# Attention outputs stored from GpSimd's queue, two outputs kept on chip, earlier loads for the first merges

## The chip, the cores and the metric

The kernel runs on one core of a Trainium2 chip. A core has TensorE (PE; PEld is its weight load), VectorE (DVE), ScalarE (ACT) and GpSimd (POOL), which work side by side and wait for each other through semaphores. SyncE (SP) only issues transfers between the chip's memory (HBM) and the on-chip buffers; GpSimd and ScalarE can issue them too. The metric is the device time of one execution in microseconds, the median of several runs.

## The reference

A hybrid decoder block on one sequence of 1024 tokens, width 1024. Queries, keys and values for 24 heads of 64, the convolution's input and two gates come from one projection. The part that the change touches:

```python
DILATED_GROUPS = ((128, 1), (512, 4), (2048, 16))     # three groups of 8 heads

outs, lses = [], []
for g, (window, dilation) in enumerate(DILATED_GROUPS):
    o_g, lse_g = dilated_group_attention(q[:, :, g], k[:, :, g], v[:, :, g], tab, window, dilation)
    outs.append(o_g)
    lses.append(lse_g)
alpha = jax.nn.softmax(jnp.stack(lses, axis=0), axis=0)
o = jnp.einsum('gbsh,gbshd->bshd', alpha, jnp.stack(outs, axis=0))
return o.reshape(B, S, ATTN_OUT_W) @ w_attn_out

u = layer_norm(u, g_ln, b_ln)          # after the depthwise convolution
return silu(u) @ w_conv_out + b_conv_out

merged = sigmoid(z_ga) * y_attn + sigmoid(z_gc) * y_conv
x = x + rms_norm(merged @ w_mix_out, g_post_mix)
h = rms_norm(x, g_pre_ffn)
x = x + rms_norm((silu(gate) * up) @ w_ffn_out, g_post_ffn)    # gate, up = split(h @ w_ffn_in)
```

Every head of the three groups attends along its own dilation, and the three groups' outputs for the same head slot are added with weights from their softmax denominators.

## The kernel before, in words

All matrix products are float32 work done in parts: an operand is split into a rounded high part (ScalarE, a cast) and the low remainder (VectorE or GpSimd, a subtraction), and three products are added. The helper `both` makes such a split with L195 (high part, ScalarE) and L196 (low part); `unit` (L305, L307, L309) issues the three products, tile by tile, for the projections between 840 and 1000 us.

The stages, by the profile's time: the input projections and the Winograd form of the convolution run to about 590 us; the norm after the convolution lies beside their end. From there the value projections (L948 to L952) run, with the attention interleaved, to about 870 us together with the first units of the convolution's output projection. The other units of that projection run to 941 us; each is evicted by L1576 and stored to an HBM buffer `dgc` by L1578, from which L1559 loads it. The attention's output projection follows (evictions L1603), then the mixing projection (L1638), the FFN's input (L321 to L323), and its output (L1909).

The attention works through 12 units, one for each head pair `hp` (0 to 3) and group `g` (0 to 2), in the order g0 for hp 0 and 1, g1 for hp 0 and 1, g2 for hp 0 and 1, and then the same for hp 2 and 3. A unit has 8 steps, one per 128 tokens. A step issues the scores (`att_s`, L1048, bias and maximum on VectorE in L1051), a step behind it the exponentials (`att_e`, L1061), then the transposes (`att_t`, L1086, with copies by L1093 on ScalarE and L1094 on VectorE) and the products with the values (`att_p`, L1121), copied into an output tile `O` by L1141. The stages of a step lag: products come 5 steps after their scores, so that the last product of a unit lies in the next unit. Within a unit GpSimd does the values' low part (`value_parts`, L918 and L922, at steps 4 and 5) and duplicates the next unit's queries onto the other half of the partitions (`double`, L886 and L887, first half at step 6, second half at step 7; the first half is read from the next unit's step 0, the second from its step 4).

When a unit's `O` is complete, L1145 stores it (512 KB, tensor `datt`, one for each g and hp) 3 ticks later, through SP's queue. The softmax statistics of groups 0 and 1 are stored after the last exponential of a unit by `tokens_out` (L1070: 1024 pieces of 16 bytes; L1072: 256 pieces of 64 bytes; tensor `dst`), also on SP, and read back in another order by L891 for the last group's unit.

With group 2 done, a generator `merge(hp, st)` starts. It makes the three groups' weights, stores them (tensor `dw`, L1184) and, once allowed, loads the three outputs (L1193, 512 KB each, in a `b` buffer) and the weights spread over the partitions (`spread`, L1154, two transfers of 256 KB each). It multiplies each output by its weights (L1204, L1208, L1216), adds (L1212, L1221) and splits the sum with `both` (L195, L196) as the operand of the attention's output projection. Until the change a merge's loads wait for the end of the attention (`self.fine is not None`) and for their turn, and four merges follow each other.

The order of the work is written by generators. TensorE's code calls `tick` after every three matmuls; `tick` runs the steps that `later(n, ...)` put n ticks ahead, and advances each background generator (`bg`), which pauses with `yield n` for n ticks. `beat` advances the attention, 0.42 steps of its generator per matmul (0.8 in the convolution's output units). Each engine, and SP's queue, then works strictly in the order written; an instruction that waits holds everything behind it. There are 42 buffers of 4 KB per partition (`b`) and a ring of 3 (`d`) for the outputs `O` and others; a load waits until the readers of the buffer's earlier content are done.

`conv_norm` subtracts the mean from the 8 channel blocks, sums the squares (L1270), makes the reciprocal deviation (`rstd`) and scales. Its steps pause 3 ticks each; when it ends, `normed` becomes 9 and the attention may begin.

Of the kernel before, what the change touches and what calls it, by code (L numbers as in the profile page):

```python
# [62 lines left out]
class Build:  # L63
# [910 lines left out]
    def attention(self):  # L974

        live, s, total = {}, 0, 96
        order = [(g, 2 * hg + i) for hg in range(2) for g in range(3) for i in range(2)]
        nxt, cur, u, x, V = self.stacks(*order.pop(0)), None, 8, None, None
        for i in range(5):
            self.stack_load(nxt)  # L980
        second = self.stacks(*order.pop(0))

        def there():
            return nxt[1] // 2 * 3 + nxt[0] < self.vn

        while s < total + self.LP:
            if s < total:
                if x is None and nxt and there():
                    x = self.values(*nxt[:2])
                if u == 8:  # L990
                    while self.normed < 9 or x is None:
                        if second and second[5] < min(5, self.normed - 4):
                            self.stack_load(second)
                        if x is None and there():
                            x = self.values(*nxt[:2])
                        yield 0
                    if cur is None:
                        self.double(nxt, 0)
                        self.double(nxt, 1)
                    cur, u, nxt, V = nxt, 0, None, []  # L1000
                live[s] = a = {}
                self.att_s(a, cur, V, u)
                u += 1

                if u in (4, 5):
                    if len(V) < 2:
                        V.append(self.value_parts(x, u - 4))
                    if u == 5:
                        x = None
                if u == 6 and cur[0] == 2:  # L1010
                    self.other_stats(cur)
                if u in (6, 7) and nxt:
                    self.double(nxt, u - 6)
                if u == 8:
                    cur[2] = cur[3] = V = None
                if u == 1:
                    if second:
                        nxt, second = second, None
                    elif order:
                        nxt = self.stacks(*order.pop(0))  # L1020
                if nxt and nxt[5] < 5:
                    self.stack_load(nxt)
            if 0 <= s - 1 < total:
                self.att_e(live[s - 1])
            yield 0
            if 0 <= s - self.LT < total:
                self.att_t(live, s - self.LT)
                yield 0
            if 0 <= s - self.LP < total:
                yield from self.att_p(live, s - self.LP)  # L1030
            s += 1
# [34 lines left out]
    def tokens_out(self, g, dst, src):  # L1066

        if g == 0:
            d = dst.rearrange("(u p) e -> p u e", p=128)
            self.nc.sync.dma_start(d, src)  # L1070
        else:
            self.nc.sync.dma_start(dst.rearrange("(b p c) e -> p b (c e)", b=2, c=4),  # L1072
                                   src.rearrange("p (b c) e -> p b (c e)", b=2))

    def att_t(self, live, k):
# [21 lines left out]
    def att_p(self, live, k):  # L1097


        nc = self.nc  # L1100
        a, b, hh = live[k & ~1], live[k | 1], k & 1
        g, hp, u = a["g"], a["hp"], a["u"]
        if hh == 0:
            a["o"] = self.bank("o")
        ps = a["o"]
        hi, lo = a.pop(("pt", hh))

        if g == 2:
            todo = [(u, 0, 128, 0), (u + 1, 128, 128, 128)]
        else:  # L1110
            n = 256 + 128 * (len(a["blocks"]) > 1)
            todo = [(u, 0, 256, 0)] + [(u - 1, 256, 128, 0)] * (n > 256) + [(u + 1, n, 128, 128)]
        for j, (kb, x, n, q) in enumerate(todo):
            kb = self.place(g, kb)
            v, w = a["V"][kb // 4]
            c = (kb % 4) * 256 + hh * 128
            vh = v[:, c:c + 66]
            vl = v[:, c + 64:c + 130] if c < 896 else w
            o = ps[0:66, hh * 256 + q:hh * 256 + q + n]
            for i, (y, z) in enumerate(((vh, hi), (vl, hi), (vh, lo))):  # L1120
                nc.tensor.matmul(o, y, z[:, x:x + n], start=i == 0 and j == 0, stop=i == 2 and j == len(todo) - 1,  # L1121
                                 skip_group_check=True)
            if j < 2:
                yield 0
        hi = lo = v = w = vh = vl = y = z = None
        if hh == 0:
            return
        if u == 0:
            self.O = self.ring()

        O = self.O
        e = (8, 2, 128)[g]
        if g == 0:
            d = O.rearrange("p (c m) -> p m c", c=8)[:, u * 16:u * 16 + 32]
        elif g == 1:
            d = O.rearrange("p (e c m) -> p c m e", e=2, c=4)[:, u // 2]
        else:
            d = O[:, u * 128:u * 128 + 256].rearrange("p (c m) -> p c m", c=2)
        for h in range(2):
            x = ps[0:64, h * 256:(h + 1) * 256]  # L1140
            nc.vector.tensor_copy(d[h * 64:(h + 1) * 64], x.rearrange("p (a e) -> p a e", e=e))  # L1141
        a["o"] = ps = d = x = O = None
        del live[k - 1], live[k]
        if u == 6:
            self.later(3, lambda x=self.O: nc.sync.dma_start(self.d_att[g, hp], x))  # L1145
            if g == 2:
                self.merges.append(self.bg(self.merge(hp, a["p"][4])))
            self.O = None

    def spread(self, hp, g):  # L1150
# [4 lines left out]
                tensor=d.tensor, offset=d.offset + (2 * g + e) * T, ap=[[0, 64], [1, T]]))  # L1155
        return x

    def merge(self, hp, st):

        nc = self.nc  # L1160
        yield 2
# [2 lines left out]
        w = t[:, 32:80].rearrange("p (g u e) -> p g u e", g=3, u=8)  # L1164
# [20 lines left out]
        t = None  # L1185
        yield 4

        while self.fine is not None or hp > self.turn:
            yield 0

        def load(g):
            y = self.slot()
            nc.sync.dma_start(y, self.d_att[g, hp])  # L1193
            return y
# [6 lines left out]
        yield 1  # L1201
        w = self.spread(hp, 1)
        yield 7
        nc.vector.tensor_tensor(y, y, x, op=OP.mult)  # L1204
        x = None
        x = self.spread(hp, 2)
        yield 1
        nc.vector.tensor_tensor(z, z, w, op=OP.mult)  # L1208
        w = None
        w = load(2)  # L1210
        yield 1
        nc.vector.tensor_tensor(y, y, z, op=OP.add)  # L1212
        z = None
        self.turn += 1
        yield 9
        nc.vector.tensor_tensor(w, w, x, op=OP.mult)  # L1216
        x = None
        yield 2
# [5 lines left out]
        yield 2  # L1224
        self.OT[hp] = self.both(z)

    turn = weighed = 0

    def split(self, src, n):
        nc = self.nc  # L1230
# [9 lines left out]
    def conv_norm(self):  # L1240
        nc = self.nc
        mean = self.slot()
        A = []

        def load():
            A.append(self.slot())
            nc.sync.dma_start(A[-1], self.d_conv[len(A) - 1])

        for _ in range(4):
            load()  # L1250
        yield 3
        for hf in range(2):
            s = slice(hf * H, (hf + 1) * H)
            ps = self.bank("s")
            nc.tensor.matmul(ps, self.mean_col.to_broadcast([128, 128]), self.csum[:, s], start=True, stop=True)
            nc.scalar.copy(mean[:, s], ps)
        self.csum = None
        yield 1
        q = []
        for b in range(10):  # L1260
            if b < 4:
                load()
            if b < 8:
                nc.vector.tensor_tensor(A[b], A[b], mean, op=OP.subtract)
            if 0 < b < 9:
                q.append(self.slot())
                nc.scalar.activation(q[-1], A[b - 1], AF.Square)
            if b > 2:
                p = q.pop(0)
                nc.vector.tensor_tensor(q[0], q[0], p, op=OP.add)  # L1270
            p = None
            yield 3
        mean = None
        yield 3
        pb = yield from self.rstd(q[0], T, self.eps_ln, 6)
        rs = self.slot()
        for hf in range(2):
            nc.scalar.copy(rs[:, hf * H:(hf + 1) * H], pb[hf])
        q = None
        for b in range(9):  # L1280
            if b < 8:
                nc.vector.tensor_tensor(A[b], A[b], rs, op=OP.mult)
            if b:
                a, A[b - 1] = A[b - 1], None
                nc.scalar.activation(a, a, AF.Silu, bias=self.col(C_BLN + b - 1), scale=self.col(C_GLN + b - 1))
                self.later(3, lambda b=b, a=a: nc.sync.dma_start(self.d_act[b - 1], a))
                a = None
                self.normed = b
            yield 1
        yield 9  # L1290
        self.normed = 9

    room = False
# [731 lines left out]
```

## Time and profile before

| | us |
|---|---|
| median of 3 runs | 1733.52 (1730.94 to 1735.8) |
| the profiled execution | 1729.18 |
| its span, first to last instruction | 1727.4 |
| TensorE busy | 1699.1 (98%) |
| VectorE, ScalarE, GpSimd busy | 1252.3, 790.1, 462.2 |
| mean granted clock of TensorE | 0.994 |

The rows of a profile name the engine, the line of the kernel, the operation and what it writes and reads (`b<-datt`: from the tensor `datt` into a `b` buffer). A count stands behind an x. In the rows on waits, "A <- B" says that A was idle until B was done. The waits are inferred: where an instruction waits for several things, the one that came last by the profile is named. A row of a window has, for each engine, the busy time and the count of instructions, then the granted clock, the mean busy share of the 16 DMA engines and what they moved.

### The profile page before, as it was taken

How to read it: one execution, taken by the hardware profiler on the slowest of the kernel's cores; microseconds unless marked ns; L12 is line 12 of the kernel's file. 1: busy time of each engine (PE TensorE's matmuls, PEld its weight loads, DVE VectorE, ACT ScalarE, POOL GpSimd, SP SyncE). 2: the span in 40 equal slices, each digit the busy share in tenths (PEclk: the TensorE clock that was granted, in tenths of full speed). 3: DMA queues.
4: the chain of work that ended last, by engine and by line, in shares of the span. 5: the costliest groups of instructions: out<-in, count | busy, mean ns of one | idle time of the engine just before them, and what ended most of it. 6: DMA issues, size and time to landing. Idle time of an engine off the chain costs nothing.

```text
span 1727.4 us, 24529 instructions
## 1 busy us (share of the span) xinstructions
PE 1699.1 (98%) x8758; PEld 1442.1 (83%) x8758; DVE 1252.3 (72%) x2214; ACT 790.1 (46%) x1550; POOL 462.2 (27%) x365
## 2 busy tenths in 40 slices
PE   8999999999999999999998999999999999999998
PEld 7788888888888999999786888888888888888886
DVE  6789978889997657677766755676556555677586
ACT  6344343344444566667622346643333333454463
POOL 0017778887885123434200120000000000000000
PEclk9999999999999999999999999999999999999999
DMA  4352434545578797888789732223322332395244
GB/s 164 111 174 88 156 116 140 160 169 183 169 188 214 223 250 207 234 219 227 224 242 321 272 125 92 90 73 110 129 92 92 110 109 92 135 362 161 92 141 153
DMA packets 167991, 285.52 MB, mean 165 GB/s; under 512 B 52434, under 2 KB 83853, under 8 KB 167869
## 3 DMA queue, kind: packets, MB, share of 16 engines
q1 hardware_dynamic: 167468, 283.46, 52.1%
q8 instruction: 69, 1.13, 0.3%
q14 instruction: 54, 0.43, 0.1%
q10 hardware_dynamic: 288, 0.27, 0.0%
q0 software_dynamic: 112, 0.24, 0.0%
HBM read 192.15 MB, written 96.47 MB: 167 GB/s over the span
## 4 chain that ended last, share of the span: by engine, by line
PE 89%; DMA 7%; DVE 1%; ACT 1%; POOL 1%; issue 1%; SPq 1%; DVEq 0%; ACTq 0%; POOLq 0%
PE p L321 15%; PE p L322 15%; PE p L323 15%; PE p L1909 12%; PE p L1638 5%; PE p L305 4%; PE p L307 4%; PE p L309 3%; PE p L1121 3%; DMA b<-datt 2%; PE p L948 2%; PE p L950 2%; PE p L952 2%; PE p L1048 2%; PE p L556 2%; PE p L1086 2%
## 5 line engine op out<-in xcount | busy, mean ns | idle before, releaser
L321 PE MATMUL p<-b,b 128*128 128x512 f32 x1204 | 469.1, 390 | 0.3 <-ACT c L340 0.3
L322 PE MATMUL p<-b,b 128*128 128x512 f32 x1204 | 468.8, 389 | 0.0
L323 PE MATMUL p<-b,b 128*128 128x512 f32 x1204 | 468.8, 389 | 0.0
L321 PEld LDWEIGHTS p<-b,b 128*128 128x128 f32 x1204 | 226.1, 188 | 48.0 <-ACT c L340 0.7
L322 PEld LDWEIGHTS p<-b,b 128*128 128x128 f32 x1204 | 226.1, 188 | 46.8
L323 PEld LDWEIGHTS p<-b,b 128*128 128x128 f32 x1204 | 226.1, 188 | 46.6
L1909 PE MATMUL p<-b,b 128*128 128x512 f32 x924 | 209.6, 389 | 0.0
L1909 PEld LDWEIGHTS p<-b,b 128*128 128x128 f32 x924 | 173.5, 188 | 35.9
L686 DVE SCALAR_TENSOR_TENSOR p<-b,par,p 128x511 f32<-128x511 f32 (+14 forms) x232 | 163.4, 738 | 0.0
L305 PE MATMUL p<-b,b 128*128 128x512 f32 x368 | 148.3, 403 | 7.7 <-ACT b L195 6.6
L309 PE MATMUL p<-b,b 128*128 128x512 f32 x368 | 147.2, 400 | 1.0 <-DVE b L189 1.0
L307 PE MATMUL p<-b,b 128*128 128x512 f32 x368 | 147.0, 399 | 0.5 <-DVE b L196 0.5
L195 ACT CAST b<-d 128x1024 fp32r<-128x1024 f32 x86 | 90.4, 1051 | 105.1 <-POOL d L216 55.1
L196 POOL TENSOR_TENSOR b<-d,b 128x1024 fp32r<-128x1024 f32 x44 | 106.9, 2429 | 79.7 <-ACT b L195 72.4
L196 DVE TENSOR_TENSOR b<-d,b 128x1024 fp32r<-128x1024 f32 x42 | 51.3, 1222 | 101.0 <-ACT b L195 101.0
L948 PE MATMUL p<-b,b 128*128 128x256 f32 x384 | 113.3, 295 | 0.0
L950 PE MATMUL p<-b,b 128*128 128x256 f32 x384 | 112.5, 293 | 0.0
L952 PE MATMUL p<-b,b 128*128 128x256 f32 x384 | 112.4, 293 | 0.0
L1233 DVE TENSOR_TENSOR b<-b,b 128x512 fp32r<-128x512 f32 x133 | 91.8, 695 | 21.1 <-ACT b L1232 18.9
L1232 ACT CAST b<-b 128x512 fp32r<-128x512 f32 x133 | 82.2, 619 | 46.2 <-PE p L1909 18.1
L1121 PE MATMUL p<-c,b 128*66 128x128 f32 (+1 forms) x620 | 87.0, 243 | 6.0 <-DVE c L1094 3.1
L1061 ACT ACTIVATE c<-c,stat 128x128 f32<-128x128 f32 (+1 forms) x192 | 85.1, 447 | 10.2 <-DVE stat L1051 9.7
(229 smaller groups left out, 2996.2 us busy)
## 6 DMA issues: line engine op xcount, KB each, us to landing
b<-w_in SPq DMA_DIRECT2D x30, 512.0 KB, 5.1
dk<-c SPq DMA_DIRECT2D x48, 256.0 KB, 3.0
dq<-c SPq DMA_DIRECT2D x48, 256.0 KB, 3.7
b<-dq SPq DMA_DIRECT2D x48, 256.0 KB, 6.1
b<-dk SPq DMA_DIRECT2D x48, 256.0 KB, 7.3
b<-w_fi SPq DMA_DIRECT2D x24, 512.0 KB, 4.8
d<-w_in SPq DMA_DIRECT2D x23, 512.0 KB, 5.1
dqS<-c SPq DMA_DIRECT2D x44, 256.0 KB, 2.2
```

The costliest lines, as they stand in the source:

```text
L196: self.wsplit.tensor_tensor(lo, x, f(hi), op=OP.subtract)
L305: nc.tensor.matmul(ps, hi[:, s], a, start=kt == 0, stop=False)
L307: nc.tensor.matmul(ps, hi[:, s], b, start=False, stop=False)
L309: nc.tensor.matmul(ps, lo[:, s], a, start=False, stop=kt == nk - 1)
L321: nc.tensor.matmul(ps, hi[:, s], a, start=first and kt == 0, stop=False, skip_group_check=True)
L322: nc.tensor.matmul(ps, hi[:, s], b, start=False, stop=False, skip_group_check=True)
L323: nc.tensor.matmul(ps, lo[:, s], a, start=False, stop=kt == 3, skip_group_check=True)
L686: nc.vector.scalar_tensor_tensor(A[i][:, j:], src[i][:, :H - j], w[i], A[i][:, j:], op0=OP.mult, op1=OP.add)
L948: nc.tensor.matmul(o, a, hi[:, s], start=kt == 0, stop=False)
L950: nc.tensor.matmul(o, a, lo[:, s], start=False, stop=False)
L952: nc.tensor.matmul(o, b, hi[:, s], start=False, stop=kt == KT - 1)
L1909: nc.tensor.matmul(acc[t], x, y, start=first and e == 0, stop=last and e == 2, skip_group_check=True)
```

## The change

It has four parts. The output tiles are stored from GpSimd's queue, one tick after completion, and the statistics too. For group 2 of head pairs 2 and 3 the output is not stored: the tile is handed to the merge, which multiplies it in place. The merges' loads no longer wait for the end of the attention, but for the beginning of its last unit (`ending`); merge 1's loads may follow merge 0's at once (`turn`), while the arithmetic still waits for the attention's end and for the merge before (`done`). The norm's sums pause 3 and 2 ticks by turns, and its last pause has 11 ticks.

```diff
                     cur, u, nxt, V = nxt, 0, None, []
+                    self.ending = s == total - 8
...
         if g == 0:
             d = dst.rearrange("(u p) e -> p u e", p=128)
-            self.nc.sync.dma_start(d, src)
+            self.nc.gpsimd.dma_start(d, src)
         else:
-            self.nc.sync.dma_start(dst.rearrange("(b p c) e -> p b (c e)", b=2, c=4),
+            self.nc.gpsimd.dma_start(dst.rearrange("(b p c) e -> p b (c e)", b=2, c=4),
...
         if u == 6:
-            self.later(3, lambda x=self.O: nc.sync.dma_start(self.d_att[g, hp], x))
+            kept = g == 2 and hp > 1
+            if not kept:
+                self.later(1, lambda x=self.O: nc.gpsimd.dma_start(self.d_att[g, hp], x))
             if g == 2:
-                self.merges.append(self.bg(self.merge(hp, a["p"][4])))
+                self.merges.append(self.bg(self.merge(hp, a["p"][4], self.O if kept else None)))
...
-        while self.fine is not None or hp > self.turn:
+        while not self.ending or hp > self.turn:
             yield 0
...
         w = self.spread(hp, 1)
         yield 7
+        self.turn += hp == 0
+        while self.fine is not None or hp > self.done:
+            yield 0
         nc.vector.tensor_tensor(y, y, x, op=OP.mult)
...
-        w = load(2)
+        w = load(2) if last is None else last
+        last = None
         yield 1
         nc.vector.tensor_tensor(y, y, z, op=OP.add)
         z = None
-        self.turn += 1
+        self.turn += hp > 0
         yield 9
+        self.done += 1
         nc.vector.tensor_tensor(w, w, x, op=OP.mult)
...
-            yield 3
+            yield 3 - b % 2
         mean = None
         yield 3
...
             yield 1
-        yield 9
+        yield 11
         self.normed = 9
```

In the changed kernel the lines behind the first edit are numbered one to ten higher. GpSimd's order in the attention, from one unit's value parts to the next unit's, before:

```order
L922 CAST vx_274<-b_5937 128x64
L886 CAST b_5760<-b_5760 64x512
L887 CAST b_5761<-b_5761 64x512
L886 CAST b_5804<-b_5804 64x512
L887 CAST b_5805<-b_5805 64x512
L886 CAST b_5760<-b_5760 64x512
L887 CAST b_5761<-b_5761 64x512
L886 CAST b_5804<-b_5804 64x512
L887 CAST b_5805<-b_5805 64x512
L918 TENSOR_TENSOR b_6242<-b_5979,b_6242 128x8x64
```

and after:

```order
L922 CAST vx_274<-b_5918 128x64
L886 CAST b_5739<-b_5739 64x512
L887 CAST b_5740<-b_5740 64x512
L886 CAST b_5783<-b_5783 64x512
L887 CAST b_5784<-b_5784 64x512
L1149 DMA datt_214<-d_5688 128x1024
L886 CAST b_5739<-b_5739 64x512
L887 CAST b_5740<-b_5740 64x512
L886 CAST b_5783<-b_5783 64x512
L887 CAST b_5784<-b_5784 64x512
L1071 DMA dst_243<-stat_5081 128x8x4
L918 TENSOR_TENSOR b_6223<-b_5954,b_6223 128x8x64
```

The store of an output came between the first and the second half of the duplication, and the store of statistics behind it, ahead of the next unit's value parts.

SP's order at the attention's last unit, before:

```order
L1145 DMA datt_221<-d_8764 128x1024
L891 DMA stat_8820<-dst_245 128x32
L891 DMA stat_8820<-dst_249 128x32
L1145 DMA datt_224<-d_9101 128x1024
L177 DMA b_9467<-w_co 128x1024
L1559 DMA b_9469<-dgc_124 128x1024
L1578 DMA dgc_121<-b_8799 128x1024
L1193 DMA b_9518<-datt_214 128x1024
L1184 DMA dw_240<-mrg_9382 48x128
L1145 DMA datt_225<-d_9368 128x1024
```

and after:

```order
L1197 DMA b_9129<-datt_214 128x1024
L1158 DMA b_9174<-dw_238 64x1024 x2
L1197 DMA b_9213<-datt_218 128x1024
L1158 DMA b_9256<-dw_238 64x1024 x2
L891 DMA stat_8795<-dst_245 128x32
L891 DMA stat_8795<-dst_249 128x32
L1197 DMA b_9418<-datt_215 128x1024
L1158 DMA b_9449<-dw_239 64x1024 x2
L1197 DMA b_9473<-datt_219 128x1024
L1158 DMA b_9495<-dw_239 64x1024 x2
L1158 DMA b_9513<-dw_238 64x1024 x2
L177 DMA b_9517<-w_co 128x1024
```

The stores of outputs (`datt_221`, `datt_224`, `datt_225`) are gone from SP's order, and the first two loads and spreads of merges 0 and 1 stand ahead of the `w_co` load that follows the attention. SP's order at the last merge, before:

```order
L177 DMA b_9843<-w_ao 128x512
L1559 DMA b_9845<-dgc_128 128x1024
L1154 DMA b_9882<-dw_241 64x1024 x2
L1578 DMA dgc_126<-b_9670 128x1024
L1193 DMA b_9900<-datt_225 128x1024
L177 DMA b_9923<-w_ao 128x512
```

and after:

```order
L177 DMA b_9777<-w_co 128x1024
L1569 DMA b_9779<-dgc_127 128x1024
L1158 DMA b_9795<-dw_241 64x1024 x2
L1588 DMA dgc_125<-b_9608 128x1024
L177 DMA b_9853<-w_ao 128x512
L1569 DMA b_9855<-dgc_128 128x1024
```

The last merge's last transfer is now the spread of `dw_241`, and it stands ahead of `dgc_128` and of the first `w_ao` load; before, `datt_225` stood behind both.

More of the change, by code (lines that the diff above doesn't have):

```diff
@@ L1156, in spread, with merge @@
         return x
-    def merge(self, hp, st):
+    def merge(self, hp, st, last):
         nc = self.nc
@@ L1225, in merge @@
         self.OT[hp] = self.both(z)
-    turn = weighed = 0
+    turn = weighed = done = 0
+    ending = False
     def split(self, src, n):
```

## The prediction

> **What bounds the kernel now.** I read the waits of TensorE first, then its work in windows, then the chain of waits before the longest stall. TensorE is busy for 98% of the span, so 28.3 us of idle time are all that can be won directly. Its longest waits (engine, line, what released it: total us, times, longest):
>
> ```profile
> PE 1699.1 (98%) x8758; PEld 1442.1 (83%) x8758; DVE 1252.3 (72%) x2214; ACT 790.1 (46%) x1550; POOL 462.2 (27%) x365
> PE p L305 <- ACT b L195: 6.6, 1, 6.6
> PE p L1121 <- DVE c L1094: 3.1, 2, 2.9
> PE p L1121 <- ACT c L1093: 2.8, 2, 2.5
> ```
>
> The first is the attention output projection, waiting for the last merge's high part. The other two are probability-times-value products inside the attention. A wait costs more than its idle time where the clock drops behind it, so I cost each stall by matmuls done per window (columns: busy us and count of PE, PEld, DVE, ACT, POOL; granted clock; DMA share; GB/s):
>
> ```profile
> 600.00:620.00 20.00, 20.00 (x169) 19.98 (x168) 10.56 (x22) 14.32 (x23) 0.00 (x0) 1.00 0.98 288
> 620.00:630.00 10.00, 7.38 (x52) 6.94 (x51) 5.04 (x20) 7.46 (x24) 8.22 (x12) 0.86 1.03 354
> 835.00:850.00 15.00, 12.15 (x69) 9.98 (x68) 9.21 (x31) 6.64 (x25) 2.62 (x5) 0.77 0.92 271
> 850.00:855.00 5.00, 5.00 (x39) 4.21 (x38) 3.96 (x15) 4.26 (x17) 2.16 (x3) 1.00 0.02 3
> 855.00:860.00 5.00, 3.87 (x25) 2.91 (x24) 3.65 (x14) 3.38 (x14) 1.26 (x2) 1.00 0.16 64
> 870.00:875.00 5.00, 5.00 (x38) 4.08 (x37) 3.44 (x8) 1.62 (x5) 0.00 (x0) 1.00 0.01 3
> 880.00:935.00 55.00, 55.00 (x245) 45.46 (x244) 35.38 (x35) 10.40 (x15) 0.00 (x0) 1.00 1.04 297
> 935.00:950.00 15.00, 7.00 (x26) 4.82 (x25) 9.73 (x11) 3.61 (x7) 0.74 (x1) 0.82 1.03 377
> 950.00:980.00 30.00, 30.00 (x130) 24.71 (x130) 22.48 (x37) 9.90 (x22) 4.54 (x6) 0.97 0.81 298
> ```
>
> Undisturbed, the last phase does 245 matmuls in 55 us, 4.45 per us. From 935 to 980 it did 156, worth 35.0 us, in 45: the merge stall costs **10.0 us**, of which 8 are idle and the rest is the clock of 0.82 and 0.97 behind it. In the same way 620 to 630 did 52 at an undisturbed 169/20 = 8.45 per us (6.15 us): **3.9 us** lost. 835 to 850 did 69 at 38 per 5 us (9.1 us): **5.9 us** lost, at a clock of 0.77. 855 to 860 did 25 (3.3 us): **1.7 us** lost. Together 21.5 us, 1.2% of the span.
>
> The chain of waits shows what the merge stall hangs on (start, us, what), and TensorE's own rows its two edges:
>
> ```profile
> by line: DMA b<-datt 56.4%; DMA b<-dgc 16.5%; DMA b<-dw 12.4%; DVE b L1221 2.7%; issue 2.2%; PE p L307 2.0%; DVE b L196 1.7%; ACT b L195 1.5%; PE p L309 1.2%; DVE b L1576 1.0%; SPq L177 1.0%; PE p L305 1.0%; SPq L1559 0.7%; DVE b L1216 0.1%
> 881.18 8.96 DMA b<-dw
> 933.76 8.99 DMA b<-datt
> 940.92 0.39 PE L309 MATMUL p<-b,b 128*128 128x512 f32 x1
> 947.86 0.80 PE L305 MATMUL p<-b,b 128*128 128x512 f32 x1 [6.55 <-ACT b L195]
> ```
>
> From 881 to 942.75, 85% of this chain is one transfer releasing the next: merge loads (`datt`, `dw`) and the spill loads `dgc`, with the DMA share at 1.03 to 1.04. The last merge's last load lands at 942.75, and the chain from there (L1216, L1221, L195) takes 5.1 us to 947.86. TensorE ran out of other work at 941.3. So the stall is a queue of bytes, not of arithmetic.
>
> **The change part by part.** (a) *Early loads of merges 0 and 1, and two kept outputs.* Transfers concerned (KB each, median us to landing):
>
> ```profile
> datt<-d SPq DMA_DIRECT2D x12, 512.0 KB, 4.5
> b<-datt SPq DMA_DIRECT2D x12, 512.0 KB, 9.7
> b<-dw SPq DMA_DIRECT2D x24, 256.0 KB, 11.0
> dst<-stat SPq DMA_DIRECT2D x8, 16.0 KB, 8.5
> ```
>
> 880 to 950 moved 55 x 0.297 + 15 x 0.377 = 22 MB, 314 GB/s. Each of merges 0 and 1 now issues two loads and two spreads (2 x 0.52 + 4 x 0.26 = 2.1 MB) during the last unit. The windows show where the room is: 3 GB/s from 850 to 855, 64 to 860, 3 from 870 to 875. Keeping two outputs takes out two loads and two stores, 2.1 MB, half of it loads in the crowded stretch. So 4.2 + 1.0 = 5.2 MB leave it: 5.2/0.314 = about 17 us of transfer. The last load would land near 926, the merge's end near 931, ten us ahead of 941.3. Bounds: if only half of the early loads get out in time and the rest of the queue keeps its pace, 3.1 MB or 10 us, still ahead by three; so I take the full 10.0 us. The lower bound is nothing (second rival). The kept output is multiplied in its own buffer by the same instruction (L1216), at no cost.
>
> (b) *Stores from GpSimd's queue.* On SP they held up what stood behind them (same columns as the first fence, between 580 and 1000), and two rows of SP's own timeline show an instance:
>
> ```profile
> SPq L1070 <- ACT c L1061: 21.1, 4, 7.6
> SPq L1145 <- DVE d L1141: 16.2, 7, 4.7
> SPq L1145 <- DVE stat L1051: 15.4, 3, 11.8
> SPq L1072 <- ACT c L1061: 12.6, 3, 4.8
> 858.42 0.32 SPq L1145 DMA_DIRECT2D datt<-d  x1
> 858.83 0.38 SPq L177 DMA_DIRECT2D b<-w_co  x1
> ```
>
> 65 us of SP's waits were for outputs not yet computed. The `w_co` weights issued at 858.83, straight after a store that had waited up to 11.8 us while DMA was empty; that is the 855 to 860 loss, and I count 1.5 of its 1.7 us as won.
>
> The two attention stalls have a DMA behind them as well, by their first late instruction:
>
> ```profile
> 623.93 0.62 ACT L188 CAST b<-b 128x512 fp32r<-128x512 f32 x1 [1.03 <-DMA dact<-b]
> 836.54 0.62 ACT L188 CAST b<-b 128x512 fp32r<-128x512 f32 x1
> 837.53 0.87 DVE L189 TENSOR_TENSOR b<-b,b 128x512 fp32r<-128x512 f32 x1 [2.55 <-ACT b L188]
> ```
>
> At 623.93 a weight split waited for a buffer that a `dact` store still read. At 837.53 VectorE had idled 2.55 us, and the ACT cast named had ended 0.4 us earlier; what it waited for last, I read, was the buffer of a `dgc` store under full DMA. Both stretches run at a DMA share of 1.0. In the changed order both buffer reuses lie farther apart, and the loads behind SP's store waits go out earlier; but no byte leaves these stretches, and a faster TensorE asks for the next bytes sooner. Bounds: 0 (both come back elsewhere) to 9.8 us. I take half, 5 us.
>
> GpSimd's side. Issuing costs what GpSimd's own DMAs cost, bounded by rows with 128 and 32 pieces, and its idle time covers it (start, us, instruction, idle before):
>
> ```profile
> L426 POOL DMA_DIRECT2D ident<-p_ident x1 | 0.7, 688 | 0.8 <-POOLq L2017 0.8
> L456 POOL DMA_DIRECT2D c<-p_tab x1 | 0.5, 511 | 0.0
> 656.36 0.37 SPq L1070 DMA_DIRECT2D dst<-stat  x1
> 664.45 1.29 POOL L918 TENSOR_TENSOR b<-b,b 128x512 fp32r<-128x512 f32 x1 [12.24 <-ACT b L917]
> ```
>
> An output store (128 rows) should take 0.7 us. It stands between the two halves of the next heads' duplication (L886, L887); behind it are four copies which the scores need only at the next unit's fifth step. The unit's steps are some 2.5 us, so about 10 us remain. A statistics store can issue when the last exponentials are done (656.36), and the next work behind it, L918, starts at 664.45: 8 us of cover. Its first form has 128 x 8 = 1024 pieces of 16 bytes. The two rows give (688 - 511)/96 = 1.8 ns a piece, so 0.5 + 1024 x 0.0018 = 2.3 us; hidden. The lower bound is 0.5; the upper bound, should a tiny piece cost like a whole short transfer, is some 15 us (fourth case).
>
> (c) *Norm in fewer steps.* The sums take 5 ticks fewer, the last pause 2 more: the attention starts 3 ticks earlier. It removes no work from TensorE and no instruction from any engine. TensorE is full there with other matmuls:
>
> ```profile
> 575.00:600.00 25.00, 25.00 (x213) 25.00 (x212) 10.29 (x15) 11.20 (x16) 8.14 (x8) 1.00 0.60 170
> ```
>
> So 0 us. A tick is three matmuls, here 3 x 25/213 = 0.35 us: a sum that came too late would cost at most the 5 ticks, 2 us.
>
> (d) *New stalls.* The early loads take buffers earlier, and stores now compete with loads inside full stretches: one 512 KB store ahead of a load is 0.5/0.314 = 1.7 us. I allow 1.5 us, between 0 and 4.
>
> **Sum**: -10.0 - 5 - 1.5 + 1.5 = -15 us. On the profiled execution's 1729.18 that is 1714; the median shown is 1733.52, 4.3 higher, so I forecast **1718.5**. The case's own range, from the bounds of (b) and (d), is 1712 to 1723.
>
> **Rivals.** *Only the queue of merge loads shortens.* The attention stalls stay or move, since full DMA and not SP causes them: -10 - 1.5 + 1.5, about 1723.5. For it: the DMA share of 1.03 at 620 to 630. Against it: the 65 us of waits at SP's head. The Trainium skill, "DMA: Bandwidth & Descriptors", section "Issuing engines are not separate DMA queues", says that transfers from any issuing engine share the same 16 engines and that issuing from several only saves the issuer's time, which it calls usually small. By that rule this rival's time holds; here the saved part is the waiting at the queue's head, not the 0.33 us of an issue.
>
> *The merge stall is replaced.* The last spread of `dw` or the conv-out spill loads come no sooner, because SP's loads wait for free buffers rather than for bytes, and the last merge lands less than 6 us earlier: -4 to -5, some 1729, no change that can be told. For it: the early loads hold their buffers from the last unit on. Against it: the chain's rows, which are all DMA and hardly SP.
>
> *Slower: GpSimd's queue becomes the bound.* If a statistics store occupies GpSimd beyond its 8 us cover, L918 is late, and with it the value operands of L1121, in each of eight units. From 8 + 15/8 = 10 us an issue the gain of 15 is eaten; at 12 us, 8 x (12 - 8) = 32 against 15 gives +17, about 1750; at 11, +9, about 1742. It takes 10 ns a piece instead of the 1.8 worked out above. The Trainium skill, "SBUF — State Buffer", section "SBUF: two separate sides", warns that a transfer from GpSimd's queue has its descriptors written by GpSimd, and that a VectorE copy within SBUF can lock it out; it measured 620 ns growing to 3100 ns. By that rule an issue of 3.1 us would still lie under the cover of 8 to 10 us; no run here shows such an overlap yet.
>
> **How the numbers follow.** Chances: the forecast 0.61, only the queue 0.15, replaced 0.13, slower 0.11. A measurement of this kernel tells some 0.3%, 5.2 us, from no change, so faster means below 1728.3. The first two cases are faster (0.76), the third the same (0.13), the last slower (0.11). The range runs from 1709 (nearly all of the 21.5 us won, with a little measurement scatter) to 1735, over the replaced case and the near end of the slower one.
>
> **What would show it.** Right: the 6.55 us before L305 is gone, windows 935 to 980 do 4.4 matmuls per us at a clock of 1.0, DMA is busy between 850 and 875, and the span from 880 to 935 has a share below 1.03. The store rows on POOL last 0.5 to 2.5 us, and L918 shows idle time before it still. Wrong: TensorE waiting for L195 or L196 at the attention output again; L1121 waiting for L918, L886 or L887; new waits on `w_co` splits (L188, L189) while early loads are in flight; or the losses at 620 and 835 unchanged, which is the first rival.

## The result, and the profile after

The changed kernel takes 1713.65 us (median; 1711.05 to 1717.3) against 1732.39 (1730.94 to 1735.8) measured beside it: a ratio of 0.9891, 95% interval 0.9866 to 0.9915. The forecast was 1718.5, in a range of 1709 to 1735. The profiled execution took 1711.05, its span 1709.1.

TensorE's waits in the changed kernel (lines behind the first edit are numbered one to ten higher: L1122 is L1121 of before, L1242 is L1232):

```profile
PE 1692.4 (99%) x8758; PEld 1437.4 (84%) x8758; DVE 1251.2 (73%) x2214; ACT 790.1 (46%) x1550; POOL 474.5 (28%) x383
PE p L556 <- ACT b L532: 5.9, 1, 5.9
PE p L305 <- ACT b L1242: 1.2, 1, 1.2
PE p L1183 <- DVE mrg L1177: 1.2, 1, 1.2
PE p L1049 <- DVE stat L1052: 0.5, 1, 0.5
```

The wait for L195 is gone, and so are the two long waits of the probability-times-value products. The wait at the start of the kernel (L556) is the same in both. The windows say the same in matmuls:

```profile
620.00:630.00 10.00, 9.46 (x81) 9.02 (x82) 7.41 (x28) 8.53 (x29) 7.47 (x12) 1.00 0.97 308
835.00:850.00 15.00, 14.88 (x109) 12.33 (x109) 12.42 (x49) 11.34 (x39) 3.04 (x4) 1.00 1.05 310
850.00:855.00 5.00, 3.71 (x23) 2.76 (x22) 3.65 (x12) 2.57 (x11) 0.00 (x0) 1.00 1.05 236
870.00:875.00 5.00, 3.78 (x18) 2.84 (x17) 4.90 (x9) 0.78 (x2) 0.00 (x0) 1.00 0.16 43
880.00:935.00 55.00, 55.00 (x244) 45.53 (x244) 36.24 (x40) 12.82 (x21) 0.95 (x1) 1.00 0.88 281
935.00:950.00 15.00, 15.00 (x68) 12.43 (x67) 11.66 (x20) 4.95 (x11) 2.21 (x3) 1.00 0.94 351
```

620 to 630 does 81 matmuls instead of 52, 835 to 850 does 109 instead of 69, 935 to 950 does 68 instead of 26, all at a clock of 1.00. DMA moved 236 GB/s from 850 to 855, where it had moved 3, and from 880 to 935 its share is 0.88 instead of 1.04. The last merge is done long before it is needed (start, us, instruction, idle before):

```profile
911.77 2.13 DVE L1230 TENSOR_TENSOR b<-b,d 128x1024 f32<-128x1024 f32 x1
913.99 1.05 ACT L195 CAST b<-b 128x1024 fp32r<-128x1024 f32 x1 [6.70 <-DVE b L1230]
```

The high part is done at 915, where the forecast had 931 and the kernel before 947.86; the first eviction of the projection that uses it (L1613, L1603 before) comes at 933.6, before at 951.1. Two small losses stand in the new profile, in the windows at 850 and at 870.

To compare many runs by place I use one measure below: in windows of 10 us, 10 minus busy time times granted clock, TensorE's lost time. The first profile of before loses 4.1 us at 620 to 640, 6.1 at 830 to 850, 1.1 at 850 to 860 and 9.6 at 930 to 960, 21.4 with a small one at 750. The changed kernel loses 1.0 at 610 to 630, 0.1 at 840 and 2.5 at 850 to 880: 3.6. The difference, 17.8, is nearly the 18.1 between the two profiled executions.

### The profile page after: what moved, and what is told of

Same layout as the page of the kernel before. It is cut to its first block, busy times and chain, and to the rows that moved or that the text cites. A ratio compares the mean times of both kernels' runs of the same rounds, so it can differ in the third digit from the quotient of the medians.

```text
span 1709.1 us, 24547 instructions
## 1 busy us (share of the span) xinstructions
PE 1692.4 (99%) x8758; PEld 1437.4 (84%) x8758; DVE 1251.2 (73%) x2214; ACT 790.1 (46%) x1550; POOL 474.5 (28%) x383
## 4 chain that ended last, share of the span: by engine, by line
PE 95%; ACT 1%; issue 1%; DVE 1%; POOL 1%; DMA 1%; SPq 0%; DVEq 0%; ACTq 0%; POOLq 0%
PE p L321 16%; PE p L323 16%; PE p L322 16%; PE p L1919 12%; PE p L1648 5%; PE p L305 5%; PE p L307 5%; PE p L309 5%; PE p L1122 3%; PE p L948 2%; PE p L950 2%; PE p L952 2%; PE p L1049 2%; PE p L556 2%; PE p L1087 2%
## 5 line engine op out<-in xcount | busy, mean ns | idle before, releaser
L321 PE MATMUL p<-b,b 128*128 128x512 f32 x1204 | 468.6, 389 | 0.3 <-ACT c L340 0.3
L323 PE MATMUL p<-b,b 128*128 128x512 f32 x1204 | 468.4, 389 | 0.0
L322 PE MATMUL p<-b,b 128*128 128x512 f32 x1204 | 468.4, 389 | 0.0
L1919 PE MATMUL p<-b,b 128*128 128x512 f32 x924 | 209.6, 389 | 0.0
L305 PE MATMUL p<-b,b 128*128 128x512 f32 x368 | 146.7, 399 | 1.3 <-ACT b L1242 1.2
L307 PE MATMUL p<-b,b 128*128 128x512 f32 x368 | 145.6, 396 | 0.0
L309 PE MATMUL p<-b,b 128*128 128x512 f32 x368 | 145.6, 396 | 0.0
L195 ACT CAST b<-d 128x1024 fp32r<-128x1024 f32 x86 | 90.4, 1051 | 105.1 <-POOL d L216 55.1
L1242 ACT CAST b<-b 128x512 fp32r<-128x512 f32 x133 | 82.1, 619 | 46.8 <-PE p L1919 18.1
L1648 PE MATMUL p<-b,b 128*128 128x512 f32 x384 | 89.4, 391 | 0.0
L195 ACT CAST b<-b 128x1024 fp32r<-128x1024 f32 x47 | 49.4, 1052 | 80.8 <-POOL b L223 37.2
```

Of the source, the lines that this page charges most:

```text
L305: nc.tensor.matmul(ps, hi[:, s], a, start=kt == 0, stop=False)
L307: nc.tensor.matmul(ps, hi[:, s], b, start=False, stop=False)
L309: nc.tensor.matmul(ps, lo[:, s], a, start=False, stop=kt == nk - 1)
L321: nc.tensor.matmul(ps, hi[:, s], a, start=first and kt == 0, stop=False, skip_group_check=True)
L322: nc.tensor.matmul(ps, hi[:, s], b, start=False, stop=False, skip_group_check=True)
L323: nc.tensor.matmul(ps, lo[:, s], a, start=False, stop=kt == 3, skip_group_check=True)
```

## The experiments

The theory behind the forecast had two causes: the bytes of the merge loads, and stores that hold up SyncE's queue in the attention. Its first rivals: the bytes alone (who issues a store doesn't matter), and phase (any shift of the attention changes which buffer is reused how soon). They were timed in three batches, each beside its own runs of the kernel before, whose medians were 1733.98, 1733.96 and 1733.67.

### One part alone

*Early loads and kept outputs.* The change without its edits to the stores' queue and the norm; against the changed kernel:

```diff
-            self.nc.gpsimd.dma_start(d, src)
+            self.nc.sync.dma_start(d, src)
...
-                self.later(1, lambda x=self.O: nc.gpsimd.dma_start(self.d_att[g, hp], x))
+                self.later(3, lambda x=self.O: nc.sync.dma_start(self.d_att[g, hp], x))
...
-            yield 3 - b % 2
+            yield 3
...
-        yield 11
+        yield 9
```

> Only the early loads and the two kept outputs; all stores stay on SyncE's queue, 3 ticks after completion, and the norm is as before. Queue theory (two causes: the merge loads' bytes, and the stores that hold up SyncE's queue in the attention): the 6.55 us before L305 is gone, the losses at 620 to 630 and 835 to 850 stay, so -10 to -11 us. Bytes theory (the attention's losses come from full DMA, and taking stores out or shifting them cures them): -17 to -19 here already. If the merge stall comes from the stores on SyncE instead, hardly anything.

Measured: 1717.21 us (1716.38 to 1717.36), ratio 0.9904 (0.9882 to 0.9927). -16.8 us, with the stores on SyncE. By place it loses nothing from 920 to 960, but 1.5 at 620 and 6.0 at 830 to 850. So nearly the whole gain comes from this part, and yet the loss at 835 stays. The bytes theory has the size, but not its reason, since the attention's losses are not cured; the second profile of the kernel before, below, shows where the size comes from.

*Stores on GpSimd's queue.*

```diff
-            self.nc.sync.dma_start(d, src)
+            self.nc.gpsimd.dma_start(d, src)
...
-            self.later(3, lambda x=self.O: nc.sync.dma_start(self.d_att[g, hp], x))
+            self.later(1, lambda x=self.O: nc.gpsimd.dma_start(self.d_att[g, hp], x))
```

> Only the stores: all twelve outputs and the eight statistics go out on GpSimd's queue, outputs one tick after completion; merges and norm as before. Queue theory: the losses at 620 to 630 and 835 to 850 go, the merge stall stays at some 6 to 7 us idle, so -7 to -9 us. Bytes theory: the same bytes go through the same 16 engines, so 0 to -1.5 us.

Measured: 1733.7 us (1730.99 to 1735.53), ratio 0.9994 (0.9981 to 1.0007). Nothing. SyncE's waits before 860 show where the 65 us went. In the kernel before three rows read:

```profile
SPq L479 <- PE p L1086: 32.2, 8, 6.2
...
SPq L870 <- PE p L1048: 2.4, 3, 1.5
SPq L871 <- PE p L1048: 2.3, 4, 0.9
```

and with the stores moved:

```profile
SPq L479 <- PE p L1086: 68.4, 9, 10.1
...
SPq L870 <- PE p L1048: 12.4, 4, 5.5
...
SPq L871 <- PE p L1048: 6.1, 4, 4.4
```

The loads behind the stores (the bias tiles of L479, the queries of L870 and L871) now wait at the queue's head for buffers that TensorE still reads, 86.9 us instead of 36.9, 50 us more. They could not have gone out earlier. What a blocking store costs here is only what the next entry could have won.

*The norm's pauses.*

```diff
-            yield 3
+            yield 3 - b % 2
...
-        yield 9
+        yield 11
```

> Only the norm's pauses. Both theories: within 2 us of the kernel before. A third theory, that the attention's two losses are a matter of phase (which buffer happens to be reused by which load) and any shift of some ticks removes or moves them: the losses at 620 and 835 change here by 3 us or more, up or down, with no store moved.

Measured: 1725.17 us (1718.7 to 1730.57), ratio 0.9950 (0.9930 to 0.9969). -8.8 us from an edit that both theories put within 2 us. In its profile, TensorE loses 0.8 us at 620 and 1.6 from 820 to 850, and 9.3 from 920 to 950. The phase theory was the one that had allowed this.

### One part undone

*The change with its stores back on SyncE*: of the diff above the first two edits, without the norm's.

> The changed kernel with its stores back on SyncE's queue, 3 ticks after completion; early loads, kept outputs and the norm as changed. Queue theory: 7 to 9 us slower than the changed kernel, -10 against the kernel before. Bytes theory: within 2 us of the changed kernel. Phase theory: differs from the run with early loads alone by 3 us or more, though only the norm's pauses differ between them.

Measured: 1715.82 us (1714.49 to 1716.91), ratio 0.9895 (0.9867 to 0.9922), beside 0.9891 (0.9866 to 0.9915) for the full change. The difference of 2 us lies inside the intervals. By place, though, the two profiles differ: this one loses 4.9 us from 820 to 850, the changed kernel 0.1. The first late instruction is a split of weights. Its load goes out at

```profile
818.74 1.65 SPq L177 DMA_DIRECT2D b<-w_co  x2
826.58 0.62 ACT L188 CAST b<-b 128x512 fp32r<-128x512 f32 x1 [2.53 <-DMA b<-w_co]
```

and in the changed kernel, where no such wait follows, 4.1 us sooner:

```profile
814.64 1.69 SPq L177 DMA_DIRECT2D b<-w_co  x2
```

With the stores on SyncE, a store of statistics stands ahead of it and goes out only at 815.98, after waiting 2.3 us for the exponentials. The other two profiles with an earlier attention and stores on SyncE (the norm's edit alone above, the start alone below) issue this load at 818.23 and 818.49 and lose 1.6 and 5.7 us from 820 to 850; the other one with an attention as early and stores on GpSimd (the first variant of the changed kernel, below) issues it at 814.77 and loses 0.1. So beside the norm's edit the stores' queue does clear this place. In the time that is some 2 us by the medians, which these runs can't tell from nothing.

*The change without the norm's edit*: of the same diff the last two.

> The changed kernel with the norm's pauses as before; early loads, kept outputs and the stores on GpSimd's queue stay. If the stores' queue is worth nothing: 1717, like the run with early loads alone. If the stores and the early loads help each other: below 1715. If the norm's pauses are worth their 9 us in any company: 1722.

Measured: 1717.11 us (1716.11 to 1718.79), ratio 0.9915 (0.9892 to 0.9937). The same as with early loads and kept outputs alone, so without the norm's edit the stores' queue is worth nothing here either. The norm's 9 us shrink in this company to 3 by the medians (1717.11 to 1713.65), and beside early loads with the stores on SyncE to 1.4 (1717.21 to 1715.82). This run's profile still loses 4.9 us from 820 to 850. It also names what the first profile had left to reading, in VectorE's waits between 820 and 850:

```profile
DVE b L189 <- DMA dgc<-b: 2.8, 1, 2.8
```

It is the `dgc` store whose buffer the weight split wants. In the kernels with the norm's edit (alone, with the early loads, and the full change) L189 has no wait between 833 and 840; the first two of them still lose 1.6 and 4.9 us from 820 to 850, at other instructions.

### What in the early loads counts, and how big the stall is

*The kernel before, profiled again*, with no edit.

> The kernel before once more, for a second profile. If the losses read from the first profile are the usual ones: 3 to 5 us at 620 to 640, 5 to 7 at 830 to 850 and 9 to 11 at 930 to 960. If they vary from execution to execution with the order of the instructions unchanged (by the run with early loads alone, which is the same program up to 840 us and lost 1.5 instead of 4.1 at 620, and by the spread of the kernel before, 1727.6 to 1738.8): one of the three differs by 3 us or more.

Measured: 1736.85 us. It loses 1.5 us at 620 (the first profile 4.1), 5.8 at 830 to 850, and 18.3 from 920 to 960 (the first profile 9.6). TensorE's waits, and the window that had carried the forecast:

```profile
PE p L305 <- ACT b L188: 5.0, 2, 2.6
PE p L305 <- ACT b L195: 4.9, 1, 4.9
PE p L309 <- DVE b L189: 3.0, 3, 1.3
```

```profile
880.00:935.00 55.00, 50.64 (x216) 40.79 (x215) 30.87 (x32) 8.79 (x13) 0.00 (x0) 0.97 1.04 257
```

The same program at the same DMA share of 1.04 moved 257 GB/s instead of 297, and the splits of `w_co` (L188, L189), whose loads stand in the same queue, were late too. This is the spread of the kernel before: its executions ran from 1721.39 to 1738.79, while the four with early loads and kept outputs lie within 1 us of each other. Four executions say little, though: the changed kernel's four lie 6 us apart.

*Outputs kept, nothing loaded early.* Against the kernel with early loads and kept outputs:

```diff
-        while not self.ending or hp > self.turn:
+        while self.fine is not None or hp > self.turn:
...
-        self.turn += hp == 0
-        while self.fine is not None or hp > self.done:
-            yield 0
```

> The kernel before with the two outputs of the last head pairs kept, and nothing else: merges load at the attention's end as before. Bytes: 2.1 MB less, 1.0 MB of it loads in the crowded stretch, 1/0.314 = 3.3 us, so the stall shrinks to 3 us idle and the time by 4 to 6 us. But the last merge also no longer waits for its last output's load at all, which was the chain's end at 942.75: if that load alone was what was late, -8 to -10.

Measured: 1723.55 us (1719.09 to 1730.16), ratio 0.9944 (0.9930 to 0.9958), -10.4. The profile, of the longest of its executions (1730.16), still waits for L195, and its chain there ends with `dw` spreads in place of the `datt` load. It loses 12.1 us from 920 to 960. By the median the stall shrinks; in this execution it stays.

*Loads early, nothing kept.* Against the same kernel:

```diff
-            kept = g == 2 and hp > 1
+            kept = False
```

> The kernel before with the early loads of merges 0 and 1, nothing kept. Bytes: 4.2 MB leave the crowded stretch, 13 us of transfer, so the stall is gone and the time falls by 9 to 16 us, as with both. If it is the kept outputs that count: -3 us or less.

Measured: 1716.36 us (1712.99 to 1716.45), ratio 0.9902 (0.9882 to 0.9923), -17.6. TensorE loses nothing from 880 to 980. The early loads suffice; the kept outputs are worth 10 us without them and nothing with them.

### What of the norm's edit counts

*Only the start of the attention.* Against the kernel before:

```diff
-        yield 9
+        yield 6
         self.normed = 9
```

> The kernel before with one number changed: the norm's last pause has 6 ticks instead of 9, its steps keep 3 each. So the attention starts 3 ticks earlier, as with the norm's edit, but the norm's sums run at their old ticks. If the start of the attention is what gains (it shifts the attention against the convolution's output units, and the reuse of the dgc store's buffer at 836 gets farther away): 1723 to 1727, as the norm's edit alone, and no wait of L189 at 836. If the shorter steps gain: 1734.

Measured: 1724.43 us (1720.12 to 1727.95), ratio 0.9958 (0.9938 to 0.9978), as with the norm's edit.

*Only the shorter steps.* Against the kernel before:

```diff
-            yield 3
+            yield 3 - b % 2
...
-        yield 9
+        yield 14
         self.normed = 9
```

> The norm's shorter steps with a last pause of 14 ticks, so that the attention starts at the same tick as in the kernel before. By the start theory 1734 and the wait of L189 at 836 as before; by the theory of the steps 1725.

Measured: 1731.53 us (1726.1 to 1736.88), ratio 0.9999 (0.9978 to 1.0019). VectorE's L189 idles 2.22 us at 834.86 and TensorE waits for it, as in the kernel before. So it is the attention's start, three ticks earlier, and not the steps. By place the start's gain is not at 835: the profile with the earlier start alone loses 5.4 us from 820 to 840 (a `dgc` load and a split of weights are late there instead), about what the kernel before lost from 830 to 850, but only 5.2 from 930 to 950. The windows from 880 to 935, first with the earlier start, then with the shorter steps:

```profile
880.00:935.00 55.00, 55.00 (x244) 45.37 (x243) 36.69 (x38) 9.82 (x14) 0.00 (x0) 1.00 1.04 305
```

```profile
880.00:935.00 55.00, 52.33 (x224) 42.36 (x223) 33.46 (x34) 10.40 (x15) 0.00 (x0) 0.97 1.04 289
```

Over the six profiles that still load all of merges 0 and 1 after the attention and keep nothing, the loss from 920 to 960 goes with these rates: 257 GB/s and 18.3 us, 284 and 15.1, 289 and 14.5, 297 and 9.6, 291 and 9.3, 305 and 5.2. That an earlier start makes the stall smaller fits this; why the rate differs, by start and by execution, no run here shows, nor which way the cause runs: a TensorE that stands still also asks for less.

### Two variants of the changed kernel

*The next merge doesn't wait for the store of weights.* In the new profile the loss at 870 is this chain, from VectorE's and TensorE's rows:

```profile
868.38 0.23 DVE L1170 TENSOR_REDUCE mrg<-stat 128x16 f32<-128x48 f32 x1 [0.93 <-DMA dw<-mrg]
872.64 0.27 PE L1183 MATMUL p<-ident,mrg 128*48 128x128 f32 x1 [1.22 <-DVE mrg L1177]
```

The one buffer `mrg` is read by the store of merge 2's weights until 868.4, and merge 3's transposition comes too late by 1.2 us.

```diff
-        nc.scalar.copy(t[0:48], ps[0:48, :128])
-        ps = None
+        h = self.half()
+        nc.scalar.copy(h[0:48, :128], ps[0:48, :128])
+        ps = t = None
...
-        nc.sync.dma_start(self.d_w[hp].rearrange("f (u p) -> (f u) p", u=8), t[0:48])
+        nc.sync.dma_start(self.d_w[hp].rearrange("f (u p) -> (f u) p", u=8), h[0:48, :128])
```

> The changed kernel, with the transposed weights of a merge copied to another buffer before they are stored, so that the next merge's first reduction (L1170 in the changed kernel) no longer waits for that store. The wait of 1.2 us before L1183 at 872 should go, -1 us, near the edge of what the runs can tell; the store holds a half buffer meanwhile, which may cost a wait in the attention, up to +2.

Measured: 1710.95 us (1710.44 to 1715.35), ratio 0.9893 (0.9863 to 0.9923). The wait is down to 0.2 us:

```profile
PE p L1183 <- DVE mrg L1177: 0.2, 1, 0.2
```

and its profiled execution is the shortest of all, 1710.44. By the ratios it can't be told from the changed kernel.

*The attention another three ticks earlier.* Against the changed kernel:

```diff
-        yield 11
+        yield 8
         self.normed = 9
```

> The changed kernel with the attention started another 3 ticks earlier (last pause 8 instead of 11). If an earlier start is good as such: -1 to -3 us. If the gain was a matter of which buffers are reused how soon after a store (phase): it may as well lose, +2 to +6, with a new wait in the attention.

Measured: 1717.82 us (1716.46 to 1719.75), ratio 0.9928 (0.9901 to 0.9955): some 4 us slower than the changed kernel by the medians. The two ratios' intervals just overlap, but all six executions are slower than all six of the variant above, timed in the same batch (1710.44 to 1715.35). So an earlier start is not good as such. It loses 3.4 us at 610 to 630 and 4.1 at 710 to 720. VectorE's wait at the second place, and TensorE's instruction behind it:

```profile
DVE d L1142 <- DMA datt<-d: 5.0, 1, 5.0
```

```profile
716.03 0.35 PE L1122 MATMUL p<-c,b 128*66 128x128 f32 x1 [2.86 <-DVE c L1095]
```

An output tile whose store had been issued by GpSimd at 706.62 was wanted for the next output. VectorE stood until 714.25, and L1095 behind it. The buffer reuse had merely moved from `dgc` to `datt`.

## Why the prediction was right or wrong

**The time** was right, and the sum of -15 close to -18.7. Its terms were not. The merge loads won 7.6 us more than their term, and of the 6.5 us counted for the stores the runs show some 2 by the medians at most: two errors that nearly cancelled, which is luck.

**(a) The merge loads: the mechanism was right, the size was not.** The stall was a queue of bytes, the early loads had room between 850 and 875, and the last merge came in time, 18 us ahead of the projection's first eviction. The term was -10.0; early loads alone measured -17.6. I had sized the stall from one execution, where it cost 9.6; the second profile of the same kernel lost 18.3 there, and the median of 1733.5 lies between. In the four profiles with this part and the attention's start as before, it is 9.6, 14.5, 15.1 and 18.3. The median stood 4.3 us above the profiled execution: that difference was carried along as if it were the same for both kernels, when by these profiles much of it was probably stall. Counting the kept outputs' 1.0 MB into the sum was needless, since the early loads do it alone.

**(b) The stores: the step that failed.** "The loads behind SP's store waits go out earlier" was read from 65 us of waits without asking what the next entries waited for; 50 us of it came back as waits of L479, L870 and L871. The sum had 6.5 us for it, 5 in the attention and 1.5 at 855. Alone the stores measured 0.9994 (0.9981 to 1.0007), and 0 against early loads alone. The rule cited for the first rival, from the Trainium skill, "DMA: Bandwidth & Descriptors", section "Issuing engines are not separate DMA queues", agrees with this measurement. The step was wrong about most of the queue, not about every entry: with the norm's edit beside it one `w_co` load did go out 4.1 us earlier, and the loss from 820 to 850 went from 4.9 to 0.1, for some 2 us in the medians that the runs can't tell from nothing. The 1.7 us at 855 to 860 weren't the `w_co` load either: the same wait, L305 for the cast of its activations on ScalarE (L1232, in the changed kernel L1242), is in every profile, at 1.0 to 1.3 us. ScalarE does the attention's work first and comes to it at 851.93 in the changed kernel, just too late.

**The attention's losses** were put at half of 9.8 us. The reading of 837.53, a `dgc` store's buffer, fits the wait that the run without the norm's edit names. The changed order did move it apart; the norm's edit, counted at 0, does that, but with the stores on SyncE the stretch then loses 1.6 and 4.9 us behind later loads. Only the two edits together clear it. The 3.9 us at 620 were an accident of the one profile: all seven further profiles with the attention's start unchanged lose 1.5 there.

**(c) The norm: the second step that failed.** "It removes no work from TensorE and no instruction from any engine" is true, but 0 us does not follow: the edit starts the attention three ticks earlier. Alone that measured -8.8, beside the early loads -1.4 to -3.5. That it shrinks so is in part because it overlaps with (a): from 920 to 960 the two profiles with the earlier start and the merge loads as before lose 9.3 and 5.2 us, the four without it 9.6 to 18.3, and the early loads remove that stall anyway.

**(d) New stalls** were put at 1.5, 0 to 4: 1.2 at 870, and the one at 850, which isn't new.

**GpSimd's side** was right. Its rows in the changed kernel between 590 and 900 (busy us, mean ns, idle before and its releasers):

```profile
L918 POOL TENSOR_TENSOR b<-b,b 128x512 fp32r<-128x512 f32 x24 | 31.0, 1294 | 122.1 <-ACT b L917 114.4 <-PE p L1122 7.6
L1149 POOL DMA_DIRECT2D datt<-d x10 | 5.6, 561 | 1.0 <-DVE d L1142 1.0
L1071 POOL DMA_DIRECT2D dst<-stat x4 | 3.7, 926 | 12.3 <-PE p L1049 6.8 <-ACT c L1062 5.5
L1073 POOL DMA_DIRECT2D dst<-stat x4 | 2.9, 735 | 13.4 <-ACT c L1062 7.3 <-PE p L1049 6.0
```

An output store holds GpSimd 0.56 us (forecast 0.7), a statistics store of 1024 pieces 0.93 (forecast 2.3), and L918 still waits 122 us in all. The fourth case had needed 10 us an issue. The growth to 3.1 us that the Trainium skill describes ("SBUF — State Buffer", section "SBUF: two separate sides") is that of a whole transfer, which the prediction took for an issue, beside a VectorE copy within SBUF. The 18 issues show none of it, at most 0.93 us each; but VectorE's copies in this stretch (L1142, `d<-p`) read TensorE's results in `p` and not SBUF, so this is no test of it.

**The rivals.** The merge stall was not replaced, and GpSimd did not become the bound. "Only the queue of merge loads shortens" was nearest to the truth on the parts: the stores alone gave nothing, and the early loads nearly everything. It had the wrong time, 1723.5, because the stall was undersized.

## What to carry to other kernels

Size a stall that hangs on full DMA from several executions: where the median lies some us above the profiled one, the stall may be larger than the profile shows. Before counting a wait at a queue's head as a gain, look at what the next entries of that queue wait for, and look again with the other edits in place. An edit that moves only the start of interleaved work has a price, because it decides how soon a buffer is reused after its store; count it among the unknown terms.

## What the runs showed that I had not expected

Moving an attention of some 250 us by three ticks changed the kernel by 9 us in one direction (1733.67 to 1724.43), and, in the changed kernel, three further ticks by some 4 us in the other (1713.65 to 1717.82, from two batches), with no work added or removed. And the DMA engines, busy with a share of 1.04, moved between 257 and 305 GB/s over the same 55 us of nearly the same transfers.
